# Graph message passing by edge counts: weights applied before the counts, larger chunks, lanes two to a word, fp8 field codes

## The chip, the cores and the metric

One Trainium2 chip; the program runs on 1 of its cores. The metric is device time in microseconds (us), the median of three runs. The hardware profiler gives one profiled execution besides; its span (from the first to the last recorded instruction) is a little shorter than the device time. Engines: TensorE (PE, with PEld for its weight loads), VectorE (DVE), ScalarE (ACT), GpSimd (POOL), SyncE (SP). A name with q (SPq) is the engine's instruction queue.

## The reference

512 nodes with 1024 features, 65536 edges, a 1024 x 1024 weight matrix:

```python
src_feat = features[src]               # (65536, 1024)
msg = src_feat @ w
out = np.zeros((N, D), dtype=np.float32)
np.add.at(out, dst, msg)
```

Equal edges are interchangeable, so out = C^T (features @ w), where C[s, d] is the number of edges from s to d. C is 512 x 512. Both kernels build C on the chip with matmuls of one-hot vectors and then do two dense products. Matrix products associate: (C^T features) w and C^T (features w) are the same, apart from rounding.

## The kernel before

Each of 128 partitions holds 512 edges. One column is one edge on each partition. For a column, VectorE makes a one-hot row `so` (128 bytes: 32 words) and `do` (256 bytes: 64 words), read as fp8, and one matmul adds `so`^T `do` to a PSUM tile of 128 x 256. Bytes of different value put several 3-bit counters into one fp32 sum: each element of the tile packs eight counters, so that 128 x 256 x 8 = 512 x 512. If a counter exceeds 7 or the packed sum loses an edge, a general path is taken at the end (`lost`); with this input it isn't.

```python
CHUNKS = [32] + [64] * 7 + [32]
LANES = 8
# index transfers: first chunk, then the rest, all on SP's queue; features and w on GpSimd's
nc.sync.dma_start(src_raw[:, 0:c0, :], src_v[:, 0:c0, :])
nc.sync.dma_start(dst_raw[:, 0:c0, :], dst_v[:, 0:c0, :])
nc.sync.dma_start(src_raw[:, c0:, :], src_v[:, c0:, :])
nc.sync.dma_start(dst_raw[:, c0:, :], dst_v[:, c0:, :])
for i in range(NS):
    nc.gpsimd.dma_start(f_sb[:, i, :], f_v[i])                       # to f16
nc.gpsimd.dma_start(w_sb[:], w.rearrange("(m p) d -> p m d", p=P))   # to f16

def prep(a, b): ...      # nine VectorE operations: value and shift of each edge's codes

def lanes(a, b, on_vector):      # key - l for l in 0..7, int16: VectorE for the first chunk,
    for to, key in ((lx_t, dl_t), (kx_t, wi_t)):            # ScalarE for the others
        ...
                for l in range(LANES):
                    act.add(to[:, a:b, l], key[:, a:b], float(-l))

def onehots(a, n):               # VectorE
    so = ring.tile([P, CMAX, 32], I32, name="so", tag="so")          # ring of 3
    xo = ring.tile([P, CMAX, LANES], I32, name="xo", tag="xo", bufs=2)
    do = ring.tile([P, CMAX, 64], I32, name="do", tag="do")
    vec.scalar_tensor_tensor(xo[:, :n, :], lx_t[:, a:b, :], 0, <vd_t broadcast>,
                             op0=ALU.is_equal, op1=ALU.mult)
    for p in range(4):
        vec.scalar_tensor_tensor(so[:, :n, p*8:(p+1)*8], kx_t[:, a:b, :], p * LANES, vsb,
                                 op0=ALU.is_equal, op1=ALU.mult)
    for k in range(8):           # shift of xo, and 0x40404040
        vec.tensor_scalar(do[:, :n, k*8:(k+1)*8], xo[:, :n, :], ...)
    return so, do

def count(a, n, so, do):
    for c in range(n):
        pe.matmul(cpack_ps[:], so[:, c, :].bitcast(F8), do[:, c, :].bitcast(F8), ...)

prep(0, c0); lanes(0, c0, True)
for t, n in enumerate(CHUNKS):
    so, do = onehots(a, n)
    if t == 0:
        prep(c0, NCOLS)          # then ScalarE's lanes of all other chunks
        ...
    count(a, n, so, do)

# after the count: eight fields, cast to f16
vec.tensor_scalar(cp_i[:], cpack_ps[:], 32.0, None, op0=ALU.mult)
for i in range(NS):
    for jd in range(2):
        vec.tensor_scalar(fld[:, i, jd, :], cp_i[:], 3 * (i + 4 * jd), 7,
                          op0=ALU.logical_shift_right, op1=ALU.bitwise_and)
        (vec.tensor_copy if jd == 0 else act.copy)(ct_v[:, i, jd], fv)
# first product, features^T C: 32 matmuls of 512 columns, evacuated as f16
pe.matmul(at_ps[m][:], f_sb[:, i, mm * P:(mm + 1) * P], ct_sb[:, i, :], ...)
# the sum of all counts (5 small matmuls) and the flag `lost`
# second product with w: 64 matmuls of 512 columns; eight pieces go out
for q in range(NS):
    for h in range(2):
        for m in range(ND):
            pe.matmul(o_ps[:], at_sb[:, m, q*P:(q+1)*P], w_sb[:, m, h*512:(h+1)*512], ...)
        <ACT if h == 0 else DVE copies o_ps to out_sb>
        nc.sync.dma_start(out[...], out_sb[...])
```

(Shortened: `...` and `<...>` mark cuts.)

Of the kernel before, what the change touches and what calls it, by code (L numbers as in the profile page):

```python
# [7 lines left out]
FP = mybir.dt.float32  # L8
FPH = mybir.dt.float16
BF = mybir.dt.bfloat16  # L10
I32 = mybir.dt.int32
I16 = mybir.dt.int16
F8 = mybir.dt.float8e5
ALU = mybir.AluOpType

# [5 lines left out]
CHUNKS = [32] + [64] * 7 + [32]  # L21
CMAX = max(CHUNKS)
LANES = 8
# [3 lines left out]
def kernel(  # L27
# [18 lines left out]
    ring_ctx = tc.tile_pool(name="mp_ring", bufs=3)  # L46
    ring = ring_ctx.__enter__()
    psum = ctx.enter_context(tc.tile_pool(name="mp_psum", bufs=8, space=bass.MemoryType.PSUM))
    ctx.enter_context(tc.manual_schedule())

    vec, act, pe = nc.vector, nc.scalar, nc.tensor
# [6 lines left out]
    c0 = CHUNKS[0]  # L58
    nc.sync.dma_start(src_raw[:, 0:c0, :], src_v[:, 0:c0, :])
    nc.sync.dma_start(dst_raw[:, 0:c0, :], dst_v[:, 0:c0, :])  # L60
    nc.sync.dma_start(src_raw[:, c0:, :], src_v[:, c0:, :])
    nc.sync.dma_start(dst_raw[:, c0:, :], dst_v[:, c0:, :])
# [5 lines left out]
    for i in range(NS):  # L68
        nc.gpsimd.dma_start(f_sb[:, i, :], f_v[i])  # L69
    w_sb = sb.tile([P, ND, D], FPH, name="w_sb")  # L70
    nc.gpsimd.dma_start(w_sb[:], w.rearrange("(m p) d -> p m d", p=P))

    ones = sb.tile([P, NCOLS], I32, name="ones")
    vec.memset(ones[:], 1)
    lane = sb.tile([P, LANES], I16, name="lane")
    for l in range(LANES):
        vec.memset(lane[:, l:l + 1], l)
# [4 lines left out]
    e_t = sb.tile([P, NCOLS], I32, name="e_t")  # L82
    vs_t = sb.tile([P, NCOLS], I32, name="vs_t")
    vd_t = sb.tile([P, NCOLS], I32, name="vd_t")
    wi_t = sb.tile([P, NCOLS], I16, name="wi_t")
    dl_t = sb.tile([P, NCOLS], I16, name="dl_t")
    kx_t = sb.tile([P, NCOLS, LANES], I16, name="kx_t")
    lx_t = sb.tile([P, NCOLS, LANES], I16, name="lx_t")

    def prep(a, b):  # L90
        s, d = src_raw[:, a:b, 0], dst_raw[:, a:b, 0]
        s16 = src_raw[:, a:b, :].bitcast(I16)[:, :, 0]
        d16 = dst_raw[:, a:b, :].bitcast(I16)[:, :, 0]

        vec.tensor_scalar(u_t[:, a:b], d, 1, 16, op0=ALU.logical_shift_right, op1=ALU.bitwise_and)  # L95
        vec.tensor_scalar(sh_t[:, a:b], s, 3, 3, op0=ALU.bitwise_and, op1=ALU.logical_shift_left)
        vec.scalar_tensor_tensor(u_t[:, a:b], s, 12, u_t[:, a:b],  # L97
                                 op0=ALU.bitwise_and, op1=ALU.bitwise_or)
        vec.tensor_scalar(e_t[:, a:b], d, 31, None, op0=ALU.bitwise_and)
        vec.tensor_scalar(u_t[:, a:b], u_t[:, a:b], 3, 36, op0=ALU.mult, op1=ALU.add)  # L100
        vec.tensor_tensor(vd_t[:, a:b], ones[:, a:b], e_t[:, a:b], op=ALU.logical_shift_left)  # L101
        vec.tensor_tensor(vs_t[:, a:b], u_t[:, a:b], sh_t[:, a:b], op=ALU.logical_shift_left)
        vec.tensor_scalar(wi_t[:, a:b], s16, 4, None, op0=ALU.logical_shift_right)
        vec.tensor_scalar(dl_t[:, a:b], d16, 6, None, op0=ALU.logical_shift_right)  # L104

    def lanes(a, b, on_vector):

        n = b - a
        for to, key in ((lx_t, dl_t), (kx_t, wi_t)):
            if on_vector:  # L110
                vec.tensor_tensor(
                    to[:, a:b, :],
                    key[:, a:b].unsqueeze(2).broadcast_to([P, n, LANES]),
                    lane[:].unsqueeze(1).broadcast_to([P, n, LANES]),
                    op=ALU.subtract)
            else:
                for l in range(LANES):
                    act.add(to[:, a:b, l], key[:, a:b], float(-l))  # L118

    cpack_ps = psum.tile([P, 256], FP, name="cpack_ps", tag="ps", padded_shape=[P, 512])  # L120

    def onehots(a, n):
        b = a + n
        so = ring.tile([P, CMAX, 32], I32, name="so", tag="so")
        xo = ring.tile([P, CMAX, LANES], I32, name="xo", tag="xo", bufs=2)
        do = ring.tile([P, CMAX, 64], I32, name="do", tag="do")
        vec.scalar_tensor_tensor(  # L127
            xo[:, :n, :], lx_t[:, a:b, :], 0,
            vd_t[:, a:b].unsqueeze(2).broadcast_to([P, n, LANES]),
            op0=ALU.is_equal, op1=ALU.mult)  # L130
        vsb = vs_t[:, a:b].unsqueeze(2).broadcast_to([P, n, LANES])
        for p in range(32 // LANES):
            vec.scalar_tensor_tensor(  # L133
                so[:, :n, p * LANES:(p + 1) * LANES], kx_t[:, a:b, :], p * LANES, vsb,
                op0=ALU.is_equal, op1=ALU.mult)
# [20 lines left out]

    a = 0
    prep(0, c0)
    lanes(0, c0, True)
    for t, n in enumerate(CHUNKS):  # L160
        so, do = onehots(a, n)
        if t == 0:
            prep(c0, NCOLS)
            a2 = c0
            for n2 in CHUNKS[1:]:
                lanes(a2, a2 + n2, False)
                a2 += n2
        count(a, n, so, do)
        a += n

    ring_ctx.__exit__(None, None, None)


    cp_i = sb.tile([P, 256], I32, name="cp_i")
    vec.tensor_scalar(cp_i[:], cpack_ps[:], 32.0, None, op0=ALU.mult)  # L175
    ct_sb = sb.tile([P, NS, N_NODES], FPH, name="ct_sb")
    ct_v = ct_sb.rearrange("p i (l jd jb b) -> p i jd b l jb", l=8, jd=2, jb=4, b=8)
    fld = sb.tile([P, NS, 2, 256], I32, name="fld")
    for i in range(NS):
        for jd in range(2):  # L180
            vec.tensor_scalar(fld[:, i, jd, :], cp_i[:], 3 * (i + 4 * jd), 7,  # L181
                              op0=ALU.logical_shift_right, op1=ALU.bitwise_and)
            fv = fld[:, i, jd, :].rearrange("p (b l jb) -> p b l jb", b=8, l=8, jb=4)
            if jd == 0:
                vec.tensor_copy(ct_v[:, i, jd], fv)  # L185
            else:
                act.copy(ct_v[:, i, jd], fv)  # L187

    over = sb.tile([P, 256], I32, name="over")
    over_b = sb.tile([P, 256], BF, name="over_b")  # L190
    vec.tensor_scalar(over[:], cp_i[:], 24, None, op0=ALU.logical_shift_right)
    vec.tensor_copy(over_b[:], over[:])
    one_h = sb.tile([P, 1], FPH, name="one_h")
    big_b = sb.tile([P, 1], BF, name="big_b")
    vec.memset(one_h[:], 1.0)
    vec.memset(big_b[:], -4194304.0)


    at_sb = sb.tile([P, ND, N_NODES], FPH, name="at_sb")
    for mh in range(2):  # L200
        at_ps = [psum.tile([P, N_NODES], FP, name=f"at_ps{mh}{m}", tag="ps") for m in range(4)]
        order = [(i, m) for i in range(NS) for m in range(4)] if mh == 0 else \
                [(i, m) for m in range(4) for i in range(NS)]
        for i, m in order:
            mm = mh * 4 + m
            pe.matmul(at_ps[m][:], f_sb[:, i, mm * P:(mm + 1) * P], ct_sb[:, i, :],  # L206
                      start=(i == 0), stop=(i == NS - 1), skip_group_check=True)
        for m in range(4):
            mm = mh * 4 + m
            if m % 2 == 0:  # L210
                vec.tensor_copy(at_sb[:, mm, :], at_ps[m][:])  # L211
            else:
                act.copy(at_sb[:, mm, :], at_ps[m][:])  # L213


    sum_ps = psum.tile([1, N_NODES], FP, name="sum_ps", tag="ps")
    for i in range(NS):
        pe.matmul(sum_ps[:], one_h[:], ct_sb[:, i, :], start=(i == 0), stop=False,  # L218
                  skip_group_check=True)
    pe.matmul(sum_ps[:, 0:256], big_b[:], over_b[:], start=False, stop=True,  # L220
              skip_group_check=True)
    sum_row = sb.tile([1, N_NODES], FP, name="sum_row")
    sum_1 = sb.tile([1, 1], FP, name="sum_1")
    act.activation(sum_row[:], sum_ps[:], mybir.ActivationFunctionType.Copy, accum_out=sum_1[:])
    lost = sb.tile([1, 1], I32, name="lost")
    vec.tensor_scalar(lost[:], sum_1[:], float(E), None, op0=ALU.not_equal)


    for q in range(NS):
        out_sb = sb.tile([P, D], FP, name=f"out_sb{q}", tag="out_sb", bufs=4)  # L230
        for h in range(2):
            o_ps = psum.tile([P, 512], FP, name="o_ps", tag="ps")
            for m in range(ND):
                pe.matmul(o_ps[:], at_sb[:, m, q * P:(q + 1) * P],  # L234
                          w_sb[:, m, h * 512:(h + 1) * 512],
                          start=(m == 0), stop=(m == ND - 1))
            if h == 0:
                act.copy(out_sb[:, h * 512:(h + 1) * 512], o_ps[:])  # L238
            else:
                vec.tensor_copy(out_sb[:, h * 512:(h + 1) * 512], o_ps[:])  # L240
# [95 lines left out]
```

## Time and profile before

| | |
|---|---|
| device time, three runs | 112.23, 111.75, 112.52 us |
| span of the profiled execution | 111.2 us |
| PE busy | 85.3 us (77%), 613 matmuls |
| DVE busy | 64.2 us (58%), 172 instructions |
| ACT busy | 45.8 us (41%), 143 instructions |
| mean granted clock of TensorE | 0.933 |
| HBM read, written | 7.34 MB, 2.10 MB |

In the rows of groups, `L148 PE MATMUL cpack_ps<-do,so` is line, engine, operation, result and operands; then come shapes, count, busy us and mean ns of one, and the idle time of the engine before them with what ended it. Instructions of one engine overlap a little in the records, so a mean can be longer than the spacing from one start to the next. A matmul's mean contains its pipeline; its rate is read from how many start in a stretch. A line of the chain of waits is start, length and what held the end during it. In a windows table each line is a stretch with busy us, number of instructions, granted clock (1.00 is full), share of DMA, GB/s. Lines of the views follow in the prediction.

### The profile page before, as it was taken

How to read it: one execution, taken by the hardware profiler on the slowest of the kernel's cores; microseconds unless marked ns; L12 is line 12 of the kernel's file. 1: busy time of each engine (PE TensorE's matmuls, PEld its weight loads, DVE VectorE, ACT ScalarE, POOL GpSimd, SP SyncE). 2: the span in 40 equal slices, each digit the busy share in tenths (PEclk: the TensorE clock that was granted, in tenths of full speed). 3: DMA queues.
4: the chain of work that ended last, by engine and by line, in shares of the span. 5: the costliest groups of instructions: out<-in, count | busy, mean ns of one | idle time of the engine just before them, and what ended most of it. 6: DMA issues, size and time to landing. Idle time of an engine off the chain costs nothing.

```text
span 111.2 us, 1643 instructions
## 1 busy us (share of the span) xinstructions
PE 85.3 (77%) x613; PEld 62.6 (56%) x613; DVE 64.2 (58%) x172; ACT 45.8 (41%) x143; POOL 3.4 (3%) x9
## 2 busy tenths in 40 slices
PE   0008940069999999999999999999179999999800
PEld 0006620046888888888888888888033434444300
DVE  2996725999999999999694900000891620222100
ACT  4000299999999999920000000000293542201200
POOL 6600000000000000000000000000000000000000
PEclk9999997555999999999999999999985999999997
DMA  1999999600000000000000000000000000434520
GB/s 28 186 315 227 211 212 213 120 3 0 0 6 0 0 0 0 6 0 0 0 0 6 0 0 0 0 6 0 0 0 0 0 0 0 189 129 160 193 99 3
DMA packets 3354, 6.42 MB, mean 58 GB/s; under 512 B 528, under 2 KB 528, under 8 KB 3344
## 3 DMA queue, kind: packets, MB, share of 16 engines
q0 software_dynamic: 1616, 3.15, 15.8%
q1 hardware_dynamic: 1728, 3.15, 7.5%
q8 instruction: 6, 0.10, 0.4%
q14 instruction: 4, 0.03, 0.1%
HBM read 7.34 MB, written 2.10 MB: 85 GB/s over the span
## 4 chain that ended last, share of the span: by engine, by line
PE 70%; DVE 10%; DMA 7%; ACT 6%; SPq 1%; issue 1%
PE cpack_ps L148 49%; PE o_ps L234 13%; PE at_ps L206 7%; DMA dst_raw<-in_dst_dram 7%; DVE so L133 2%; ACT lx_t L118 2%; ACT ct_sb L187 2%; DVE do L139 2%; ACT kx_t L118 2%; PE sum_ps L218 1%; DVE ct_sb L185 1%; DVE out_sb L240 1%; DVE vd_t L101 1%; DVE u_t L97 1%; DVE cp_i L175 0%
## 5 line engine op out<-in xcount | busy, mean ns | idle before, releaser
L148 PE MATMUL cpack_ps<-do,so 128*128 128x256 fp8e5 x512 | 61.4, 287 | 16.7 <-DVE do L142 16.7
L148 PEld LDWEIGHTS <-so 128*128 128x128 fp8e5 x512 | 52.5, 103 | 25.3 <-DVE so L133 12.7
L118 ACT ACTIVATE lx_t<-dl_t 128x64 int16<-128x64 int16 (+1 forms) x64 | 20.9, 760 | 11.2 <-DVE dl_t L104 11.2
L133 DVE SCALAR_TENSOR_TENSOR so<-kx_t,vs_t 128x512 int32<-128x512 int16 (+1 forms) x36 | 20.3, 627 | 4.5 <-PE cpack_ps L148 2.9
L118 ACT ACTIVATE kx_t<-wi_t 128x64 int16<-128x64 int16 (+1 forms) x64 | 21.2, 769 | 0.0
L139 DVE TENSOR_SCALAR do<-xo 128x512 int32<-128x512 int32 (+1 forms) x63 | 20.0, 391 | 0.0
L187 ACT CAST ct_sb<-fld 128x256 f16<-128x256 int32 x4 | 4.6, 1356 | 32.0 <-DVE fld L181 32.0
L234 PE MATMUL o_ps<-w_sb,at_sb 128*128 128x512 f16 x64 | 14.0, 379 | 0.0
L206 PE MATMUL at_ps<-ct_sb,f_sb 128*128 128x512 f16 x32 | 8.9, 442 | 3.1 <-ACT ct_sb L187 3.0
L234 PEld LDWEIGHTS <-at_sb 128*128 128x128 f16 x64 | 6.2, 98 | 7.6 <-issue 0.3
L240 DVE COPY out_sb<-o_ps 128x512 f32<-128x512 f32 x4 | 2.8, 692 | 11.0 <-PE o_ps L234 11.0
L175 DVE TENSOR_SCALAR cp_i<-cpack_ps 128x256 int32<-128x256 f32 x1 | 0.4, 425 | 14.3 <-PE cpack_ps L148 14.3
L206 PEld LDWEIGHTS <-f_sb 128*128 128x128 f16 x32 | 3.6, 111 | 8.3 <-issue 5.8
L127 DVE SCALAR_TENSOR_TENSOR xo<-lx_t,vd_t 128x512 int32<-128x512 int16 (+1 forms) x9 | 5.6, 626 | 2.5 <-ACT lx_t L118 2.5
L238 ACT COPY out_sb<-o_ps 128x512 f32<-128x512 f32 x4 | 2.3, 585 | 9.8 <-PE o_ps L234 9.8
L211 DVE CAST at_sb<-at_ps 128x512 f16<-128x512 f32 x4 | 2.7, 689 | 3.8 <-PE at_ps L206 3.8
L213 ACT CAST at_sb<-at_ps 128x512 f16<-128x512 f32 x4 | 2.2, 587 | 4.1 <-PE at_ps L206 4.1
L142 DVE TENSOR_SCALAR do<-xo 128x512 int32<-128x512 int32 (+1 forms) x9 | 3.5, 391 | 0.0
L185 DVE CAST ct_sb<-fld 128x256 f16<-128x256 int32 x4 | 2.9, 720 | 0.1
L181 DVE TENSOR_SCALAR fld<-cp_i 128x256 int32<-128x256 int32 x8 | 2.9, 391 | 0.0
L69 POOL DMA_DIRECT2D f_sb<-in_features_dram x4 | 2.3, 599 | 0.8 <-POOLq L320 0.8
L95 DVE TENSOR_SCALAR u_t<-dst_raw 128x32 int32<-128x32 int32 (+1 forms) x2 | 0.6, 296 | 2.3 <-DMA dst_raw<-in_dst_dram 2.3
(29 smaller groups left out, 13.8 us busy)
## 6 DMA issues: line engine op xcount, KB each, us to landing
w_sb<-in_w_dram POOLq DMA_DIRECT2D x1, 2048.0 KB, 18.5
out_dram<-out_sb SPq DMA_DIRECT2D x8, 256.0 KB, 2.1
f_sb<-in_features_dram POOLq DMA_DIRECT2D x4, 256.0 KB, 7.6
src_raw<-in_src_dram SPq DMA_DIRECT2D x1, 480.0 KB, 5.1
dst_raw<-in_dst_dram SPq DMA_DIRECT2D x1, 480.0 KB, 7.3
src_raw<-in_src_dram SPq DMA_DIRECT2D x1, 32.0 KB, 1.8
dst_raw<-in_dst_dram SPq DMA_DIRECT2D x1, 32.0 KB, 1.8
```

Of the source, the lines that this page charges most:

```text
L118: act.add(to[:, a:b, l], key[:, a:b], float(-l))
L127: vec.scalar_tensor_tensor(xo[:, :n, :], lx_t[:, a:b, :], 0, vd_t[:, a:b].unsqueeze(2).broadcast_to([P, n, LANES]), op0=ALU.is_equal, op1= ...
L133: vec.scalar_tensor_tensor(so[:, :n, p * LANES:(p + 1) * LANES], kx_t[:, a:b, :], p * LANES, vsb, op0=ALU.is_equal, op1=ALU.mult)
L139: vec.tensor_scalar(o, xo[:, :n, :], 6 - k, 0x40404040, op0=ALU.logical_shift_left, op1=ALU.bitwise_and)
L142: vec.tensor_scalar(o, xo[:, :n, :], 1, 0x40404040, op0=ALU.logical_shift_right, op1=ALU.bitwise_and)
L148: pe.matmul(cpack_ps[:], so[:, c, :].bitcast(F8), do[:, c, :].bitcast(F8), start=(a + c == 0), stop=(a + c == NCOLS - 1), skip_group_check ...
L181: vec.tensor_scalar(fld[:, i, jd, :], cp_i[:], 3 * (i + 4 * jd), 7, op0=ALU.logical_shift_right, op1=ALU.bitwise_and)
L185: vec.tensor_copy(ct_v[:, i, jd], fv)
L187: act.copy(ct_v[:, i, jd], fv)
L206: pe.matmul(at_ps[m][:], f_sb[:, i, mm * P:(mm + 1) * P], ct_sb[:, i, :], start=(i == 0), stop=(i == NS - 1), skip_group_check=True)
L234: pe.matmul(o_ps[:], at_sb[:, m, q * P:(q + 1) * P], w_sb[:, m, h * 512:(h + 1) * 512], start=(m == 0), stop=(m == ND - 1))
L240: vec.tensor_copy(out_sb[:, h * 512:(h + 1) * 512], o_ps[:])
```

## The change

It does several things at once:

- The product with w is moved ahead. Features are transposed on TensorE (32 transposes) and multiplied with w (64 matmuls of 512 columns) between chunks of the count; the evacuations are ScalarE's. After the count only C^T times the projected features is left: 32 matmuls of 512 columns or their equivalent.
- Chunks are 40, 64, 112, 104, 104, 88 columns in place of 32, seven of 64, and 32; the ring has two slots.
- Lanes: ScalarE writes two 16-bit lanes as one 32-bit word, by arithmetic (times 65537), four passes for a chunk in place of eight. `xo` of all but the first chunk is ScalarE's too (`d_words`): distance, then a power of two through the exponent bits.
- Empty matmuls (15 + 4 + 4) at the start keep TensorE at work until the first data come.
- A field of 0 to 7 is used as the fp8 code that it is (an fp8e5 with bits 0 to 7 is linear in them), as the stationary operand beside f16; no cast. The product's factor of 65536 is put in when the output is evacuated.
- The tail goes by quarters of the output rows; the counts are summed by ScalarE's accumulator.
- The transfers: indices on two queues, w in three pieces, the last two output pieces on ScalarE's queue.

The core of the diff (cuts marked by `...`; the general path, which is not taken, is left out):

```diff
-CHUNKS = [32] + [64] * 7 + [32]
+CHUNKS = [40, 64, 112, 104, 104, 88]
...
-    ring_ctx = tc.tile_pool(name="mp_ring", bufs=3)
+    ring_ctx = tc.tile_pool(name="mp_ring", bufs=2)
...
+    nc.sync.dma_start(src_raw[:, 0:ca, :], src_v[:, 0:ca, :])      # ca = 40 + 64
+    act.dma_start(dst_raw[:, 0:ca, :], dst_v[:, 0:ca, :])
+    nc.sync.dma_start(src_raw[:, ca:, :], src_v[:, ca:, :])
...
+    act.dma_start(dst_raw[:, ca:, :], dst_v[:, ca:, :])
+    pool.dma_start(f_sb[:, 0, :], f_v[0])
+    pool.affine_select(ident[:], ...)
+    for i in range(1, NS):
+        pool.dma_start(f_sb[:, i, :], f_v[i])
+    pool.dma_start(w_sb[:, 0:4, 0:512], w_v[:, 0:4, 0:512])
+    pool.dma_start(w_sb[:, 4:8, 0:512], w_v[:, 4:8, 0:512])
+    pool.dma_start(w_sb[:, :, 512:D], w_v[:, :, 512:D])
...
+    def lanes(to, key, x, k):
+        act.activation(key, x, ACTF.Copy, bias=-(0.5 - 0.5 ** (k + 1)), scale=0.5 ** k)
+        for l in range(0, LANES, 2):
+            act.activation(to[:, :, l // 2], key, ACTF.Copy,
+                           bias=-float(l + 65536 * (l + 1)), scale=65537.0)
+    def d_words(a, b):
+        act.activation(dk_t[:, a:b], e_t[:, a:b], ACTF.Copy, bias=-240.0)
+        for l in range(0, LANES, 2):
+            act.activation(z_t[:, :n, l // 2], dk_t[:, a:b], ACTF.Copy, scale=-65537.0, bias=...)
+        act.activation(far_t[:, :n], z_t[:, :n].bitcast(I16), ACTF.Abs)
+        act.activation(bits_t[:, :n], far_t[:, :n], ACTF.Relu, scale=-8388608.0, bias=top[:])
+        act.activation(xo[:, :n].bitcast(U32), bits_t[:, :n].bitcast(FP), ACTF.Copy)
...
+    def idle(n):
+        for _ in range(n):
+            pe.matmul(idle_ps[:], blank[:, 0:P], blank[:], start=True, stop=True)
+    def transposes(i):
+        for m in range(ND):
+            pe.transpose(t_ps[:, m, :], f_sb[:, i, m * P:(m + 1) * P], ident[:])
+        act.copy(ft_sb[:, :, i, :], t_ps[:])
+    def project(h, i, m0=0, m1=ND):
+        for m in range(m0, m1):
+            pe.matmul(p_ps[h, i][:], ft_sb[:, m, i, :], w_sb[:, m, h * 512:(h + 1) * 512], ...)
+    def keep(h, i):
+        act.copy(fw_sb[:, i, h * 512:(h + 1) * 512], p_ps[h, i][:])
+    s_lanes(0, c0); d_lanes(0, c0); codes(0, ca); values(0, ca); s_lanes(c0, ca)
+    xos = {1: d_words(*spans[1])}
+    idle(15); transposes(0); idle(4); transposes(1); idle(4); transposes(2)
+    so, do = onehots(0, c0)
+    count(0, c0, so, do)
+    transposes(3)
+    so, do = onehots(c0, ca - c0, xos[1])
+    s_lanes(*spans[2]); codes(ca, NCOLS); xos[2] = d_words(*spans[2])
+    s_lanes(*spans[3]); values(ca, NCOLS)
+    for i in range(NS):
+        project(0, i, 0, 4)
+    count(c0, ca - c0, so, do)
+    for i in range(NS):
+        project(0, i, 4, ND)
+        keep(0, i)
+    xos[3] = d_words(*spans[3])
+    for i in range(NS - 1):
+        if i == 2:
+            s_lanes(*spans[4])
+        project(1, i)
+        keep(1, i)
+    s_lanes(spans[5][0], NCOLS)
+    for t in range(FIRST, len(CHUNKS)):
+        so, do = onehots(starts[t], CHUNKS[t], xos[t])
+        if t + 2 < len(CHUNKS):
+            xos[t + 2] = d_words(*spans[t + 2])
+        count(starts[t], CHUNKS[t], so, do)
+        if t == FIRST + 1:
+            project(1, NS - 1, 0, LAST)
+    project(1, NS - 1, LAST, ND)
...
+    def product(q, a, b):
+        for i in range(NS):
+            pe.matmul(o_ps[q, a][:], fld[:, q, i, :].bitcast(F8)[:, 0:4 * P:4], fw_sb[:, i, a:b], ...)
+    def deliver(eng, q, a, b, queue=nc.sync):       # evacuate times 65536, and send
...
+    convert(0); fields(0); keep(1, NS - 1)
+    product(0, 0, 512); product(0, 512, D)
+    fields(1); add_up(0)
+    product(1, 0, 512); product(1, 512, D)
+    deliver(vec, 0, 0, 512); deliver(act, 0, 512, D)
+    convert(1); fields(2); add_up(1)
+    product(2, 0, 512); product(2, 512, D)
+    deliver(act, 1, 0, 512); deliver(vec, 1, 512, D)
+    fields(3); add_up(2)
...
+    product(3, 0, 512); product(3, 512, 768); product(3, 768, D)
+    deliver(act, 2, 0, 512); deliver(vec, 2, 512, D); add_up(3)
+    deliver(vec, 3, 0, 512); deliver(act, 3, 512, 768, act)
...
+    deliver(vec, 3, 768, D, act)
```

## The prediction

> **What bounds the kernel now.** I read the chain that ended last first, since it says which engine holds the end stage by stage; then the timeline around the start and after the count; then the groups, for durations.
>
> The chain of waits in order of time (start us, us, what):
>
> ```profile
> 2.13 7.29 DMA dst_raw<-in_dst_dram
> ...
> 13.18 2.47 ACT lx_t L118 x8
> 15.65 2.28 ACT kx_t L118 x8
> ...
> 17.95 2.50 DVE so L133 x4
> 20.45 2.35 DVE do L139 x7
> ...
> 23.19 54.93 PE cpack_ps L148 x480
> ...
> 79.79 2.41 ACT ct_sb L187 x2
> ...
> 82.25 7.89 PE at_ps L206 x28
> ...
> 91.20 13.93 PE o_ps L234 x64
> ...
> 105.16 0.69 DVE out_sb L240
> ```
>
> Three stretches. Until 23.19 little of TensorE's work is done: the second index transfer lands at 9.4, VectorE codes 480 columns, ScalarE writes sixteen small lane passes, and only then VectorE makes the second chunk. From 23.19 to 78.12 TensorE alone counts. From 78.12 to the end at 111.2, 33.1 us, everything is serial: fields, first product, second product, output.
>
> The timeline shows what TensorE did before the wait:
>
> ```profile
> 8.62 6.46 PE L148 MATMUL cpack_ps<-do,so 128*128 128x256 fp8e5 x32 [8.62 <-DVE do L142]
> ```
>
> So 32 columns cost 202 ns each, and after that TensorE sat idle for 8.1 us. The windows of the count (us, TensorE busy and matmuls, granted clock, DMA share, GB/s) show the price of that idle time:
>
> ```profile
> 25.00:27.00 2.00, 2.00 (x12) 0.50 0.00 0
> 27.00:28.00 1.00, 1.00 (x6) 0.50 0.00 0
> 28.00:29.00 1.00, 1.00 (x11) 0.98 0.00 0
> ...
> 33.00:40.00 7.00, 7.00 (x67) 1.00 0.00 0
> ```
>
> At half clock a column takes 167 to 200 ns; at full clock 41 of the 480 columns are done by 30.2, and the other 439 take 47.9 us, 109 ns each. So an ideal count of 512 columns is 55.9 us, and before it occupies 8.62 to 78.12, 69.5 us. The 13.6 us between are one wait and two cold starts.
>
> The groups of instructions give prices (busy us, mean ns, idle before):
>
> ```profile
> L118 ACT ACTIVATE kx_t<-wi_t 128x64 int16<-128x64 int16 x56 | 19.6, 787 | 0.0
> L133 DVE SCALAR_TENSOR_TENSOR so<-kx_t,vs_t 128x512 int32<-128x512 int16 x28 | 17.5, 686 | 3.0 <-ACT kx_t L118 1.6 <-PE cpack_ps L148 1.5
> L139 DVE TENSOR_SCALAR do<-xo 128x512 int32<-128x512 int32 x49 | 17.0, 421 | 0.0
> L187 ACT CAST ct_sb<-fld 128x256 f16<-128x256 int32 x4 | 4.6, 1356 | 32.0 <-DVE fld L181 32.0
> L238 ACT COPY out_sb<-o_ps 128x512 f32<-128x512 f32 x4 | 2.3, 585 | 9.8 <-PE o_ps L234 9.8
> ```
>
> ScalarE takes 1356 ns for 256 strided two-byte results and 585 ns for 512 contiguous four-byte ones. Means overlap, so I use start-to-start spacings from the timeline: `so` 0.61 us at 512 elements and 0.33 at 256; `do` 0.347 and 0.214. Lines through these: `so` 0.06 us + 1.06 ns an element, `do` 0.08 us + 0.52 ns.
>
> **What the Trainium skill says.** "TensorE: Matmul & The Clock Gate", Back-to-back issue gap: N/2.4 + 2.5 ns warm, N/1.2 cold. For 256 columns that is 109 and 213 ns, for 512 columns 216. The trace agrees on 109 warm, on 202 for the mostly cold first burst, and on 13.93/64 = 218 ns for o_ps. Part 1 of the same page says that about 3.4 us without work halves the clock: the trace shows it, twice here. The same page, Weight-path perf modes: fp8 without DoubleRow runs at bf16 speed; so fp8 fields buy no matmul time. "ScalarE: Activation LUTs", What ACT_TABLE_LOAD costs: 186 ns + 0.833 ns an element, overlapping by 93 ns when independent. 585 ns for 512 fits (612); the two-byte strided passes do not, they cost about 4.5 ns an element. "SBUF — State Buffer", Who interferes with whom: VectorE's two-port modes block GpSimd's descriptor generation. The before kernel has the same mix and its weights land 18.5 us after issue, so I take that as included.
>
> **The change, part by part.**
>
> *Front, to the first counted column.* Both first index pieces now hold 104 columns and go out at 0.75 on two queues; estimate landed at 3.1 (before, 32 columns landed by 2.96). ScalarE then makes two sets of 40-column lanes: each one key pass, 0.28, and four word passes, 0.6: 4.9 us. v_t to 5.2, vs_t 5.4. VectorE: xo 0.4, four `so` of 320 elements 1.6, eight `do` 2.0: ready at 9.4. But TensorE's order puts three transposes ahead. Their pieces of features landed 4.9, 7.6 (median) and 8.8 us after issues between 1.25 and 3.0; one GpSimd selection now stands between the first and the others. Estimate: third piece near 11, its eight transposes 0.7: first column at 11.5 us, which is 2.9 later than before, but on a warm array (15+4+4 empty matmuls of 512 columns since 1.3 us).
>
> *Count and projection.* Count 512 x 0.109 = 55.9. Features times weights: 64 matmuls of 512 columns, of which 60 stand before the last count: 60 x 0.216 = 13.0. Fourth transposes 0.7. If TensorE never waits, the count ends at 11.5 + 55.9 + 13.0 + 0.7 = 81.1, 3 us later than now. Does it wait? VectorE: chunks of 40, 64, 112, 104, 104, 88 columns cost (from the lines above) 4.0, 5.2, 8.4, 7.9, 7.9, 6.8, and the codes of the rest 2.2: 42 us, against 70 on TensorE. With two ring slots chunk t+2 starts when chunk t is counted. Chunk 2 is ready near 28, TensorE wants it near 35; chunk 3 ready 39, wanted 47; chunk 4 starts 47, ready 55, wanted 59; chunk 5 starts 59, ready 66, wanted 71. ScalarE by the skill's formula: d words 4.1 us and s lanes 1.1 for 104 columns, eight evacuations of 0.59, four transpose copies of 1.0: about 36 us in all. So neither should hold TensorE. Weights: 22 us before for all of them; the first quarter is wanted at 16.5 (estimate: landed 14), the last half at 30.
>
> *Tail.* Removed: the f16 cast of the fields (ct_sb), 64 matmuls of o_ps (now hidden in the count's stretch, though not free there), the at_ps evacuations, the sum matmuls in front of o_ps. Left after the last column: 4 projection matmuls 0.9 that cover conversion (0.3) and four 128-element field passes (0.2 each, estimate from the `do` line plus striding); then 32 matmuls of 512 columns' worth, 6.9. TensorE alone would end at T+8.2. VectorE holds two conversions 0.6, 16 field passes 3.3, three evacuations of 0.69 and one of half that size 0.4, reductions 0.6; with its waits I get its last evacuation at T+8.9. Before, from the last evacuation's end (105.85) to the end of the span was 5.3 us; the last piece is half as large, so 5.0. Tail 8.9 + 5.0 = 13.9 against 33.1.
>
> *Sum.* 81.1 + 13.9 = 95.0 us of span. The measured time was 112.23 for a span of 111.2, so add 1.0: **96.0 us**. The account: +2.9 front, +0.1 count and projection (69.6 against 69.5: the projection fills exactly what was idle or cold), -19.2 tail; 16.2 us less.
>
> **Rivals.**
>
> *ScalarE becomes the bound.* It takes over xo, in three passes of eight elements a column, and every lane. If the 4.5 ns an element of the strided two-byte passes held for all of these, a 104-column chunk would cost 8 x 0.47 + 3 x 3.7 = 15 us against 11.4 on TensorE, and the whole would end near 110. For it: ScalarE's slow rows. Against: the new results are four-byte and the eight-wide passes contiguous, like the 585 ns row. If only the strided lanes stay slow, a chunk is 8 us and nothing moves.
>
> *The transfers hold TensorE.* Features or weights later by 4 us (smaller rows, GpSimd's selection, VectorE's two-port work) would show as a wait at a transpose or at p_ps, and give about 100. For: three transposes stand ahead of the first count. Against: in the before profile DMA is idle after 22 us, long before the second half is wanted.
>
> *The tail is VectorE's.* Strided field passes at 0.39 instead of 0.2 add 3 us: 99. Against: 128 elements, contiguous results.
>
> *A cold array.* A gap over a window between the empty matmuls and the first column costs up to 1.7 us: 97.7. The fillers speak against it.
>
> **Range and chances.** The two large terms (55.9 and 13.0) are measured rates. Front 10 to 14, tail 12.5 to 17, and stalls in the middle 0 to 2 are the uncertain ones: 92.5 to 100.5. Only the first rival in full brings it near 112, so faster 0.97, same 0.02, slower 0.01.
>
> **What would show it.** Right: cpack_ps at 109 ns with idle time almost only before the first column; p_ps at 216 ns with no releaser; about 70 us between the first column and the last; last evacuation some 9 us after the last column; clock 1.0 from about 8 us on. Wrong: TensorE waiting for xo or kx (first rival), for features or weights (second), fld means near 0.4 us and matmuls waiting for fld (third), half clock after 10 us (fourth). If the tail is over 18 us or the first column later than 15, my sum fails there.

## The result, and the profile after

The changed kernel takes 93.75 us (median of four runs, 93.51 to 93.88) against 111.99 for the kernel before on the same chip: ratio 0.836, 95% interval 0.832 to 0.840. The prediction was 96.0, range 92.5 to 100.5. The span of the profiled execution fell from 111.2 to 92.1 us.

The chain of waits of the changed kernel, in order of time (start us, us, what):

```profile
1.43 5.87 DMA f_sb<-in_features_dram
...
7.35 0.62 PE t_ps L220 x8
7.97 0.86 PE idle_ps L211 x4
...
10.14 0.45 PE t_ps L220 x8
10.59 4.37 PE cpack_ps L198 x40
14.96 0.45 PE t_ps L220 x8
15.40 3.45 PE p_ps L229 x16
18.86 6.99 PE cpack_ps L198 x64
25.84 8.63 PE p_ps L229 x40
34.48 23.58 PE cpack_ps L198 x216
58.05 0.86 PE p_ps L229 x4
58.92 20.96 PE cpack_ps L198 x192
79.88 0.86 PE p_ps L229 x4
80.74 7.01 PE o_ps L319 x36
...
87.78 0.42 DVE o L328
```

From 7.35 to 87.75 every line is TensorE's and each begins where the last one ends. Before, the chain passed through VectorE and ScalarE ahead of 23.19, and through casts and two serial products after 78.12. Now there is one engine to read, and its total is the time. TensorE's busy time is in fact larger than before, 86.3 us against 85.3: no matmul of the count or the products has gone (96 of 512 columns and 512 of 256 are needed in both), 32 transposes and 23 empty matmuls have come; only the five small matmuls for the sum of counts, 1.0 us, have shrunk to two of one column. What went is mostly time in which TensorE waited or ran on half its clock.

The list of waits shows who still waits (engine and line waited for: us in total, times, longest us):

```profile
ACT fw_sb L233 <- PE p_ps L229: 39.6, 5, 35.6
DVE cp_i L300 <- PE cpack_ps L198: 15.0, 1, 15.0
...
DVE do L189 <- ACT xo L165: 3.1, 1, 3.1
...
PE t_ps L220 <- DMA f_sb<-in_features_dram: 0.3, 1, 0.3
```

The long waits are those of VectorE and ScalarE for TensorE, which cost nothing. VectorE once waits 3.1 us for ScalarE's xo (fourth chunk), and TensorE never notices. TensorE's only entry after its first instruction is 0.3 us for the first features.

The groups (busy us, mean ns, idle before):

```profile
L198 PE MATMUL cpack_ps<-do,so 128*128 128x256 fp8e5 x512 | 56.5, 273 | 0.0
L229 PE MATMUL p_ps<-w_sb,ft_sb 128*128 128x512 f16 x64 | 14.5, 379 | 0.0
L319 PEld LDWEIGHTS <-fld 128*128 128x128 fp8e5 x36 | 3.5, 98 | 3.7 <-issue 0.4
L306 DVE TENSOR_SCALAR fld<-cp_i 128x128 int32<-128x128 int32 x16 | 3.2, 268 | 0.1
```

Zero idle time in front of the count and of the projection. Fp8 fields load as weights in 98 ns, as f16 does, though only every fourth byte is read.

### The profile page after: what moved, and what is told of

Read it like the earlier page. It is cut to its first block, busy times and chain, and to the rows that moved or that the text cites. A ratio compares the mean times of both kernels' runs of the same rounds, so it can differ in the third digit from the quotient of the medians.

```text
span 92.1 us, 1683 instructions
## 1 busy us (share of the span) xinstructions
PE 86.3 (94%) x669; PEld 64.4 (70%) x669; DVE 50.9 (55%) x115; ACT 40.0 (43%) x103; POOL 5.3 (6%) x14
## 4 chain that ended last, share of the span: by engine, by line
PE 87%; DMA 6%; issue 1%; DVE 1%; POOLq 0%
PE cpack_ps L198 61%; PE p_ps L229 15%; PE o_ps L319 8%; DMA f_sb<-in_features_dram 6%; PE t_ps L220 2%; PE idle_ps L211 2%; DVE o L328 0%; DVE lost L368 0%; POOLq L451 0%
## 5 line engine op out<-in xcount | busy, mean ns | idle before, releaser
L198 PE MATMUL cpack_ps<-do,so 128*128 128x256 fp8e5 x512 | 56.5, 273 | 0.0
L183 DVE SCALAR_TENSOR_TENSOR so<-kx_t,vs_t 128x832 int32<-128x832 int16 (+4 forms) x24 | 19.2, 863 | 12.2 <-issue 8.7
L233 ACT CAST fw_sb<-p_ps 128x512 f16<-128x512 f32 x8 | 4.6, 591 | 39.6 <-PE p_ps L229 39.6
L189 DVE TENSOR_SCALAR do<-xo 128x832 int32<-128x832 int32 (+4 forms) x42 | 18.3, 507 | 3.1 <-ACT xo L165 3.1
L229 PE MATMUL p_ps<-w_sb,ft_sb 128*128 128x512 f16 x64 | 14.5, 379 | 0.0
L229 PEld LDWEIGHTS <-ft_sb 128*128 128x128 f16 x64 | 6.2, 98 | 6.7
L211 PE MATMUL idle_ps<-blank 128*128 128x512 f16 x23 | 7.7, 497 | 1.4 <-DVE blank L76 1.4
L319 PE MATMUL o_ps<-fw_sb,fld 128*128 128x512 f16 (+1 forms) x36 | 7.1, 355 | 0.0
L142 ACT ACTIVATE kx_t<-wi_t 128x104 int32<-128x104 int32 (+4 forms) x24 | 5.3, 356 | 0.2
L163 ACT ACTIVATE bits_t<-far_t,top 128x832 int32<-128x832 f32 (+3 forms) x5 | 4.6, 924 | 0.2
L192 DVE TENSOR_SCALAR do<-xo 128x832 int32<-128x832 int32 (+4 forms) x6 | 3.0, 507 | 0.0
## 6 DMA issues: line engine op xcount, KB each, us to landing
w_sb<-in_w_dram POOLq DMA_DIRECT2D x2, 512.0 KB, 10.4
w_sb<-in_w_dram POOLq DMA_DIRECT2D x1, 1024.0 KB, 16.4
```

Source lines behind the costliest of these rows:

```text
L142: act.activation(to[:, :, l // 2], key, ACTF.Copy, bias=-float(l + 65536 * (l + 1)), scale=65537.0)
L163: act.activation(bits_t[:, :n], far_t[:, :n], ACTF.Relu, scale=-8388608.0, bias=top[:])
L183: vec.scalar_tensor_tensor(so[:, :n, p * LANES:(p + 1) * LANES], kx, p * LANES, vsb, op0=ALU.is_equal, op1=ALU.mult)
L189: vec.tensor_scalar(o, xo[:, :n, :], 6 - k, 0x40404040, op0=ALU.logical_shift_left, op1=ALU.bitwise_and)
L211: pe.matmul(idle_ps[:], blank[:, 0:P], blank[:], start=True, stop=True)
L229: pe.matmul(p_ps[h, i][:], ft_sb[:, m, i, :], w_sb[:, m, h * 512:(h + 1) * 512], start=(m == 0), stop=(m == ND - 1))
```

## The experiments

My theory after the result: the gain is TensorE's waiting and half-clock time, filled by work that no longer follows the count; lanes, chunks and fp8 codes matter only where they let that happen. Rivals: the front (word lanes, larger chunks, transfers) carries the gain; or the new order with its short tail does. All times are medians beside runs of the kernel before on the same chip, which lay between 111.6 and 113.3 us in all. A median is that of all executions, a ratio leaves out one execution in each of two runs that was over 1.5% slower than the fastest of its kernel (106.11 us in the first run below, 111.01 us in the old kernel with empty matmuls). The tail by quarters, the summing by ScalarE and the new transfers were not undone one by one.

### The two halves apart

First the changed front with the old order of the products:

```diff
-    idle(15); transposes(0); idle(4); transposes(1); idle(4); transposes(2)
+    idle(23)
-    transposes(3) ... project(...) ... keep(...)        # all of them
-    convert(0) ... deliver(vec, 3, 768, D, act)
+    # fields, at_ps, sum and o_ps as in the kernel before
```

> The changed kernel's front (transfers, word lanes, chunks, empty matmuls) with the products in the old order and the old tail; nothing is left out. Theory, that the gain is TensorE's idle and cold time filled by work moved ahead: without the projection TensorE has counted its first 104 columns near 21.5 us, waits until about 25.5 for the third chunk and goes cold, ends the count near 72.5, and the old tail of 33 us follows: about 106.5 us. Rival, that the front (chunks, lanes) carries most of the gain: 97 or less. Rival, that the new order and tail carry all of it: 111 or more.

Measured 103.89 us, ratio 0.927 (0.920 to 0.934). TensorE's timeline (start, busy us, engine, line; in brackets the idle time before and who ended it):

```profile
14.52 7.15 PE L198 MATMUL cpack_ps<-do,so 128*128 128x256 fp8e5 x64 [0.57 <-DVE do L192]
25.11 46.37 PE L198 MATMUL cpack_ps<-do,so 128*128 128x256 fp8e5 x408 [3.44 <-DVE do L192]
74.56 7.79 PE L298 MATMUL at_ps<-ct_sb,f_sb 128*128 128x512 f16 x32 [3.09 <-ACT ct_sb L279]
```

The wait for the third chunk that the changed kernel fills with projection lies open here: 3.44 us, and the 408 columns then take 46.4 us where 44.6 would do. The count was expected to end near 72.5 and ended at 71.5. The total is about 3 us below what I expected (103.3 us in this execution), mostly because the tail was 30.2 us, not 33.1: at_ps ran at full clock (7.8 us against 9.0 before, after the same wait of 3 us in front of it), and from the last evacuation to the end of the span it took 3.6 us instead of 5.3.

Then the old front with the new order:

```diff
 # kernel before, int16 lanes, chunks of 32 and 64, old transfers
+            for i in range(NS): transposes(i)          # ahead of the first chunk's count
         count(a, n, so, do)
+        if 1 <= t <= NS: project(0, t - 1); keep(0, t - 1)
+        elif NS < t < 2 * NS: project(1, t - NS - 1); keep(1, t - NS - 1)
-    # fields, at_ps, o_ps
+    # the changed kernel's tail
```

> The kernel before with its transfers, int16 lanes and chunks, but with transposes and projection ahead (one group of eight matmuls after each chunk from the second on) and the new tail by quarters with fp8 fields; nothing is left out. Theory: the second chunk still comes at 23.3, the projection can't fill the wait before it since its weights land at 22, so the count ends near 92 (480 columns 52.4, cold 2.5, projection 13.8) and the tail is 12.3: about 105.5 us. Rival, that order and tail carry all of the gain: about 95. If both halves added up independently, the two runs of this pair would lose 18 us together; the theory expects about 12.5 together, the rest only in combination.

Measured 105.91 us, ratio 0.943 (0.937 to 0.948). TensorE's timeline:

```profile
12.70 5.23 PE L157 MATMUL cpack_ps<-do,so 128*128 128x256 fp8e5 x32
23.88 9.91 PE L157 MATMUL cpack_ps<-do,so 128*128 128x256 fp8e5 x64 [5.95 <-DVE do L151]
```

The second chunk still comes at 23.9 and its 64 columns take 9.9 us on a cold array, where 7.0 is the warm price. Neither half alone explains the change. As shares of the time before, the halves save 7.3% and 5.8%, 13.1% together, and the change saves 16.4%: the missing 3.3%, 3.7 us give or take 1.1 by the three intervals, exist only in combination; I had expected more of it, since the halves saved 14.7 us together and not 12.5. The traces show what it is made of, though no run separates it. With the new front, the new order also fills the wait of 3.44 us and saves the 1.8 us of cold columns behind it; with the old front it can't fill the wait before the second chunk. Against these 5.2 us stands above all the shorter end after the last evacuation, 1.7 us in one half and 1.1 in the other, which is counted twice in the sum of the halves.

### Cold time

```diff
 # kernel before
+    idle(17)                      # ahead of the first chunk
         count(a, n, so, do)
+        if t == 0: idle(44)       # in the wait for the second chunk
```

> The kernel before with 17 empty matmuls before its first chunk and 44 in the wait before its second. Theory: only the second cold start lies on the path (24 columns at 202 in place of 109 ns), so 2.3 us less: about 109.7 us. Rival, that the cold start is hidden behind the supply of one-hots: 112, no change. If the 44 overrun the wait, the second chunk starts later than 23.2 and some of it is lost again.

Measured 110.93 us, ratio 0.982 (0.973 to 0.992). TensorE's timeline:

```profile
8.62 3.65 PE L150 MATMUL cpack_ps<-do,so 128*128 128x256 fp8e5 x32 [0.70 <-DVE do L144]
...
23.21 52.56 PE L150 MATMUL cpack_ps<-do,so 128*128 128x256 fp8e5 x480 [1.43 <-DVE do L144]
```

The 480 columns cost 52.56 us instead of 54.93, the expected 2.4. The first chunk gets 2.8 us shorter too, and that gains nothing, since the second doesn't come before 23.2. The time's interval is wide (0.9 to 3.1 us less) and holds the expected 2.3; the gain itself is small, but clear of zero.

The other way round, the changed kernel without its 23 empty matmuls:

```diff
-    idle(15); transposes(0); idle(4); transposes(1); idle(4); transposes(2)
+    transposes(0); transposes(1); transposes(2)
```

> The changed kernel without its 23 empty matmuls. Theory: the first column comes at about 10.1 instead of 10.4, but transposes and the first 30 to 40 columns run on the half clock, 3 to 4 us more: 95.5 to 97 us. Rival, that the array warms up on the transposes alone or that the wait for features bounds the front: 93.4 us.

Measured 95.36 us, ratio 0.853 (0.848 to 0.857), some 1.7 us more than the changed kernel by the two ratios. TensorE's timeline:

```profile
8.04 1.04 PE L220 MATMUL t_ps<-ident,f_sb 128*128 128x128 f16 x8 [8.04 <-DMA f_sb<-in_features_dram]
...
10.59 1.03 PE L220 MATMUL t_ps<-ident,f_sb 128*128 128x128 f16 x8 [0.26 <-DMA f_sb<-in_features_dram]
11.41 4.72 PE L198 MATMUL cpack_ps<-do,so 128*128 128x256 fp8e5 x40
```

Direction right, mechanism half right. The columns were hardly cold: forty of them take 4.56 us to the next transpose at 15.97, 114 ns each, and only the first two take 0.2 us. The transposes were: about 0.107 us each, 0.82 a group, against 0.056 and 0.45 warm. So the first column came at 11.4, not 10.1, and the cold time ended earlier than I had put it. This profile shows only part of the 1.7 us. The unaltered kernel, run again below, had its features as late as here (first transpose at 8.05), its first column at 11.13 and a span of 92.9 us against 93.3: the cold start accounts for about 0.5 us, 0.28 before the first column and 0.2 in the two cold ones. This execution was the fastest of its four; where the rest of the median's loss lies isn't shown.

### The parts of the change one by one, undone

Fields as f16 by a cast (and output scale 1):

```diff
+    def cast(q): vec.tensor_copy(fh[:, q], fld[:, q])
     fields(0)
+    cast(0)                                  # likewise after fields(1), (2), (3)
-            pe.matmul(..., fld[:, q, i, :].bitcast(F8)[:, 0:4 * P:4], fw_sb[:, i, a:b], ...)
+            pe.matmul(..., fh[:, q, i, :], fw_sb[:, i, a:b], ...)
```

> The changed kernel with each quarter's fields cast to f16 by VectorE (128x512, int32 to f16) before the product; the output is scaled by 1 in place of 65536. Theory: the first cast, about 0.4 us, lies on the path (four projection matmuls cover 0.86 us, of which conversion and fields take 0.8), later ones mostly beside TensorE's work: 94.1 to 94.8 us. Rival, that fp8 codes speed up the product itself: its matmuls of 512 columns would go above 0.216 us and the run to 96 or more. Rival, no effect: 93.75.

Measured 95.73 us, ratio 0.854 (0.850 to 0.858): about 1.9 us more, twice what I expected. TensorE's timeline of the tail, after the last projection at 79.91:

```profile
81.86 5.34 PE L324 MATMUL o_ps<-fw_sb,fh 128*128 128x512 f16 x24 [0.92 <-DVE fh L314]
87.46 1.91 PE L324 MATMUL o_ps<-fw_sb,fh 128*128 128x512 f16 x12 [0.26 <-DVE fh L314]
```

The four casts are 0.43 us each. The first costs 0.92 us of TensorE time, not 0.4: conversion and four fields took 1.15 us (80.11 to 81.26), not 0.8, and the cast has to wait for all four, while in the changed kernel the product began at 80.66, with the first fields. Later casts are not free: VectorE is nearly full in the tail, so the last quarter's fields and the last evacuation slide too. Matmuls still take 379 ns by the mean and weight loads 98: fp8 codes save casts, not matmul time.

Lanes one by one as int16, and xo on VectorE:

```diff
-        for l in range(0, LANES, 2):
-            act.activation(to[:, :, l // 2], key, ACTF.Copy,
-                           bias=-float(l + 65536 * (l + 1)), scale=65537.0)
+        for l in range(LANES):
+            act.add(to[:, :, l], key, float(-l))            # to is int16
     def d_words(a, b):
+        d_lanes(a, b); return None                          # xo by VectorE for every chunk
...                                                          # tiles and codes to match
```

> The changed kernel with lanes one by one as int16 (eight passes a key, source and destination) on ScalarE, and xo of every chunk on VectorE, as before; order, chunks and transfers stay. Theory, that TensorE is the bound and only the front sees the lanes: first column at about 11.8 in place of 10.4, later chunks just in time: 95 to 96 us. Rival, that word lanes carry the change: TensorE waits for xo or kx at several chunks, 99 or more.

Measured 96.14 us, ratio 0.857 (0.852 to 0.861), about 2 us more. ScalarE's timeline for the 112-column chunk, first of this run, then of the changed kernel:

```profile
18.21 4.21 ACT L134 ACTIVATE kx_t<-wi_t 128x112 int16<-128x112 int32 x8
```

```profile
16.68 1.02 ACT L142 ACTIVATE kx_t<-wi_t 128x112 int32<-128x112 int32 x4
```

The same lanes cost 4.2 us as two-byte results and 1.0 as words. Yet TensorE waits for a chunk only once:

```profile
36.63 23.74 PE L191 MATMUL cpack_ps<-do,so 128*128 128x256 fp8e5 x216 [0.63 <-DVE do L185]
```

So 0.63 us of the loss is this wait; most of the rest is the front, with the first column at 11.95. VectorE's first do ended at 11.2, against 9.4 to 9.95 in the profiles of the changed kernel, but it didn't set the first column here: the features landed at 8.83, TensorE waited 2.34 us for them, and its three groups of transposes ended at 11.95. By these numbers, do at 11.2 would have been the later of the two had the features come as early as in the changed kernel. So this one profile doesn't say how much of the front is the lanes'. Word lanes are worth having, but they don't carry the change.

The old chunks:

```diff
-CHUNKS = [40, 64, 112, 104, 104, 88]
+CHUNKS = [32] + [64] * 7 + [32]
```

> The changed kernel with chunks of 32, seven of 64, and 32 in place of 40 to 112 columns; ring of two as in the change. Theory: TensorE never waits for a chunk after the first, so 93.3 to 94.2. Rival, that large chunks are what keeps VectorE ahead: 96 or more, with TensorE waiting for do.

Measured 94.01 us, ratio 0.839 (0.835 to 0.843), beside 0.836 and 0.838 for the changed kernel: the intervals overlap, no difference that I can show. TensorE's timeline:

```profile
33.72 14.14 PE L198 MATMUL cpack_ps<-do,so 128*128 128x256 fp8e5 x128
47.70 1.03 PE L229 MATMUL p_ps<-w_sb,ft_sb 128*128 128x512 f16 x4
48.56 31.60 PE L198 MATMUL cpack_ps<-do,so 128*128 128x256 fp8e5 x288
```

No bracket, so no wait. VectorE is busy 53.6 us instead of 50.9, a saving of the larger chunks that nobody waits for.

### Is TensorE the bound from end to end?

```diff
             project(1, NS - 1, 0, LAST)
+            idle(16)
```

> The changed kernel with 16 empty matmuls of 512 columns after the fourth chunk. Theory, TensorE bounds everything from 7 us on: 16 x 0.216 = 3.45 us more, 97.2 us. Rival, that another engine has the bound in the middle or the tail: less than 1.5 us more.

Measured 97.98 us, ratio 0.872 (0.868 to 0.876). The span is 96.3 against 92.9 of the unaltered kernel in the next group of runs, whose first column comes at the same 11.1 us: 3.4 us for 16 x 0.216. Time put on TensorE in the middle appears in full at the end. (The medians differ by 4.1, on different chips.)

### An earlier front

With everything else filled, only the first 10 us and the end are left. The unaltered kernel was run beside three trials:

> The changed kernel once more, unaltered, as the yardstick of the three runs beside it: 93.75 us within 0.5.

Measured 93.91 us, ratio 0.838 (0.834 to 0.842).

```diff
-    idle(15); transposes(0); idle(4); transposes(1); idle(4); transposes(2)
+    idle(15); transposes(0); idle(2); transposes(1); idle(2); transposes(2)
```

> The changed kernel with 15, 2 and 2 empty matmuls in place of 15, 4 and 4. Theory: the first column is then bound by VectorE's do near 10 us instead of TensorE's own queue at 10.4: 0.4 us less, 93.3. Rival: the features land too late for it, the two transposes wait instead, no change.

Measured 93.98 us, ratio 0.837 (0.833 to 0.841): no change. The rival holds; the first column comes at 11.06 in place of 11.13, because each group of transposes now waits for its features:

```profile
9.34 0.62 PE L220 MATMUL t_ps<-ident,f_sb 128*128 128x128 f16 x8 [0.20 <-DMA f_sb<-in_features_dram]
...
10.60 0.62 PE L220 MATMUL t_ps<-ident,f_sb 128*128 128x128 f16 x8 [0.21 <-DMA f_sb<-in_features_dram]
11.06 4.53 PE L198 MATMUL cpack_ps<-do,so 128*128 128x256 fp8e5 x40
```

So the empty matmuls stand where TensorE would wait anyway; the transfers set the front.

```diff
-CHUNKS = [40, 64, 112, 104, 104, 88]
+CHUNKS = [24, 72, 112, 104, 104, 96]
-    nc.sync.dma_start(src_raw[:, ca:, :], ...); act.dma_start(dst_raw[:, ca:, :], ...)
     pool.dma_start(w_sb[:, 0:4, 0:512], ...)
+    pool.dma_start(src_raw[:, ca:, :], ...)
+    pool.dma_start(dst_raw[:, ca:, :], ...)
     pool.dma_start(w_sb[:, 4:8, 0:512], ...)
-    idle(15); ... idle(4); ... idle(4)
+    idle(13); ... idle(1); ... idle(1)
```

> The changed kernel with a smaller first chunk (24, 72, 112, 104, 104, 96), the rest of the indices sent on GpSimd's queue behind the features and the first piece of w instead of beside the features, and 13, 1, 1 empty matmuls. Theory, that the front is the only stretch in which TensorE doesn't work for the result, and that features and the first one-hots can both come earlier: first column near 8.3 us in place of 10.4, nothing else waits: 91.6 us. Rival: the rest of the indices or of the weights now come too late, TensorE waits in the middle: 94 or more.

Measured 93.23 us (92.99 to 93.33), ratio 0.830 (0.826 to 0.833), 0.7 us better than the unaltered kernel beside it, whose six runs all lie above (93.83 to 94.57), and a third of what I hoped for. TensorE's timeline:

```profile
9.16 0.62 PE L220 MATMUL t_ps<-ident,f_sb 128*128 128x128 f16 x8 [0.63 <-DMA f_sb<-in_features_dram]
9.61 2.78 PE L198 MATMUL cpack_ps<-do,so 128*128 128x256 fp8e5 x24
...
13.03 3.61 PE L229 MATMUL p_ps<-w_sb,ft_sb 128*128 128x512 f16 x16 [0.19 <-DMA w_sb<-in_w_dram]
```

The features landed 5.5 us after issue by the median instead of 6.9, the first column came 1.5 us earlier than in the run beside it, and TensorE still waits for features and once for weights. The transfers are the limit of the front: VectorE's first do was ready at 8.6.

Last, the same with the last output piece on SP's queue:

```diff
-    deliver(vec, 3, 768, D, act)
+    deliver(vec, 3, 768, D)
```

> As the run before, and the last output piece goes out on SP's queue instead of behind another on ScalarE's. Theory: its transfer starts right after its evacuation, about 0.4 us less: 91.2 us. Rival: the end waits for the flag and the barrier, no change.

Measured 93.20 us, ratio 0.830 (0.826 to 0.834): no change, the rival holds. From the last evacuation to the end it took 4.1 us, beside 4.0 in the run before: what sets the end isn't the queue of that piece.

## Why the prediction was right

By its own steps, in us; the last column is measured minus predicted:

| step | predicted | measured | |
|---|---|---|---|
| first column | 11.5 | 10.4 | -1.1 |
| first to last column | 69.6 | 69.5 | -0.1 |
| last column to last evacuation | 8.9 | 8.3 | -0.6 |
| from there to the end of the span | 5.0 | 3.9 | -1.1 |
| span to device time | 1.0 | 1.65 | +0.65 |
| time | 96.0 | 93.75 | -2.25 |

The span was forecast 2.9 us too long, and 0.65 of that was taken back by luck, in the step from span to device time. For it I had set the median of other executions (112.23) against the span of the profiled one (111.2). Within one execution the two differ by 1.6 to 1.9 us in all runs, for example 93.82 and 92.1.

*Count and projection.* Shown. The rates of the kernel before (109 and 216 ns) added up without a wait, and 16 more matmuls cost 3.4 us. It was the largest term and the surest: a sum of measured rates on an engine that, by the ledger of the other two, is never kept waiting.

*Front.* The estimate for the third piece of features, near 11, was late by about 1 us; it was there by 9.98. That the transposes and not VectorE bound the first column was right: do was ready at 9.95 and the transposes ended at 10.43, and with fewer empty matmuls they wait for features instead. The features' landing is also the least steady term: the first piece's transposes start between 7.35 and 8.1 in profiles of the changed kernel and its near variants, so part of the 1.1 is chance (11.13 for the first column when it was run again).

*Tail.* Half of the 0.6 us is a slip in the sum: I put TensorE's own end at 8.2 us after the last column, but its terms, 0.9 and 6.9, make 7.8, and 7.87 was measured. Field passes start 0.2 us apart and hid under the four projection matmuls as predicted, and fp8 gave no matmul time. That VectorE, not TensorE, is nearly the bound there shows in the cast run.

*The end* is where a reason fell. I took 0.3 us off the 5.3 because the last piece is half as large. But the two half-changed kernels need 3.6 us (new front) and 4.2 us (new order) from the last evacuation to the end, and the first of them sends whole pieces on SP's queue, as before. What both share with the changed kernel is how the flag is read (its runtime bounds check is left out) and the general path's transfers on GpSimd's queue. No run separates the two, but the trace of the kernel before points at the second. There SP's queue steps through eight semaphores at the branch (L247, `if lost`) before it reaches the barrier at the end of the program (L331). The first line is from the list of waits of SP's queue; the others give one line's instructions with their durations in ns (least, median, most) and the first and last start in us:

```profile
SPq L247 <- SPq L247: 1.4, 1, 1.4
...
L247 SPq EVENT_SEMAPHORE  x8: 17/17/17, 107.3 to 109.1; - x8
...
L331 SPq EVENT_SEMAPHORE  x12: 17/28/28, 109.2 to 111.1; - x12
```

One of the eight ends 1.4 us after the one before it, at 108.9, just as the last output piece has landed, 3.0 us after its issue at 105.87. So the whole barrier follows that landing, and 2.3 us pass until the end; they are 2.3 in the old kernel with empty matmuls too, which has the same ending. In the three kernels with the new ending SP's eight are missing, part of the barrier's steps are done while the last piece is under way, and the end comes 1.1 to 1.2 us after the landing. That is some 1.1 us of the difference; in the run with the new front, the other 0.5 us are a faster landing (2.5 us). The bounds check was over at 107.1, before the piece had landed, so it held nothing up here.

*Rivals of the prediction.* ScalarE as the bound did not happen: eight-wide passes of 832 elements take 0.90 us, close to the 0.88 that is the estimate by the formula of the Trainium skill's page "ScalarE: Activation LUTs", What ACT_TABLE_LOAD costs, and word lanes 0.25 us for 112 elements. The 4.5 ns an element belong to two-byte strided results alone, as the int16 run shows beside the contiguous two-byte results of fw_sb (512 elements in 0.59 us). The transfers hold the front, mildly, and nothing later. Slow field passes did not occur. The half clock was kept away from 6 us on by the empty matmuls, which are worth about 1.7 us by the medians, though only 0.5 of it could be found in a profile.

*Readings that were off* without bearing on the sum: at half clock, columns start 213 ns apart in the trace of the kernel before; the 167 to 200 ns came from counting a matmul in every window that it touches. The `do` passes start 0.335 and 0.202 us apart, not 0.347 and 0.214. And the second stretch of half clock there followed only 3.0 us without matmuls (78.12 to 81.13), less than the 3.4 us that I quoted for it, and set in at 82.7, when matmuls had been running at full rate again for 1.5 us; in the run with the new front and the old order the same wait, 3.1 us, cost no clock.

*The account of the gain* in the prediction (front +2.9, middle 0, tail -19.2) has become +1.8, 0, -20.9. It holds, but must not be read as "the tail is what pays": with the new tail and order alone the kernel stands at 105.9. The tail's work moved into the middle, and the middle had room only because the front kept TensorE supplied and there was projection to fill the wait for the third chunk.

## What to carry to other kernels

Before moving work, add up the bound engine's necessary time at full rate and compare it with the span: here 512 x 0.109 + 96 x 0.216 = 77 us of matmuls stood in 111, and nearly the whole gain was in that difference, not in fewer operations. Independent work of the bound engine is worth most in a place where it would wait and, for TensorE, cool down; faster supply and moved work gained about 3.7 us together beyond what each gained alone. Once the bound engine has no gaps, finer tuning of the others (here chunk sizes, a few empty matmuls, an output queue) measures as nothing.

## What the runs showed of the hardware that was not expected

- ScalarE writes two-byte results with a stride of 16 bytes at about 4.5 ns an element (passes of 40 and 112 elements start 0.14 and 0.46 us apart) and four-byte results with the same stride at about 1.0 ns (0.13 and 0.20 us).
- How long a cold TensorE takes to reach full clock differs widely, and transposes can bring it there. Without empty matmuls, 24 transposes between 8.0 and 11.4 us, 0.107 us each, were followed by two columns of 0.2 us and then by columns of 0.109: full clock came 3.8 us after the first transpose. In the kernel with old front and new order, 24 transposes as dense (9.37 to 12.70) were followed by fifteen columns of 0.213 us, and full clock came after 6.5 us. Empty matmuls needed 4.6 us in the changed kernel and 3.3 in the one with the old order. The granted clock of the windows doesn't show the first cold start: this line of the run without empty matmuls (us, busy and matmuls, clock, DMA share, GB/s) reads 1.00 while transposes ran at half rate:

```profile
8.00:10.00 2.00, 1.75 (x15) 1.00 1.12 208
```

- The first and fastest of the features' transfers, always issued at 1.43 or 1.44 us, took 5.9 to 7.4 us to land in nine executions of the changed kernel and of the variants that issue the transfers in the same order.
